# The opening of a fused attention, pooling and FFN block, ordered by a scheduler graph

## Chip, cores and metric

The kernel runs on one core of one Trainium2 chip. The metric is the device time of one execution in microseconds (us), as the median of several runs. TensorE is called PE in the profile, VectorE DVE, ScalarE ACT, GpSimd POOL and SyncE SP. DMAs are issued by SP and ACT here.

## The reference

One layer of a decoder block on x of 1024 rows (tokens) by 1024 columns, all in float32. What matters here is its start: a norm of x's rows, and one projection of the result, of which q and k are two parts (four heads, for each 128 columns of q and 128 of k).

```python
def rms_norm(x, g):
    xf = x.astype(jnp.float32)
    y = xf * lax.rsqrt(jnp.mean(xf * xf, axis=-1, keepdims=True) + NORM_EPS)
    return (y * g.astype(jnp.float32)).astype(x.dtype)
...
    u = rms_norm(h, mix_pre_g)
    z = jnp.einsum('bsd,de->bse', u, w_in)
    ...
    p, q, k, v = z[..., :o1], z[..., o1:o2], z[..., o2:o3], z[..., o3:o4]
    gate_a, gate_b = z[..., o4:o5], z[..., o5:]
    ya = jnp.einsum('bsc,cd->bsd', pool_mixer(p, pool_mix, pool_scale), w_branch_a)
    yb = jnp.einsum('bsc,cd->bsd',
                    diff_attention(q, k, v, lam_q1, lam_k1, lam_q2, lam_k2, subln_g, lambda_init),
                    w_branch_b)
    m = jax.nn.sigmoid(gate_a) * ya + jax.nn.sigmoid(gate_b) * yb
    h = h + rms_norm(jnp.einsum('bsd,de->bse', m, w_out), mix_post_g)
...
```

## The kernel before, in words

**Products.** A float32 operand is split into a rounded part (`hi`, on ACT) and the rest (`lo`, on DVE or POOL). A product is three matmuls: hi by hi, hi by lo, lo by hi. x is loaded in eight tiles of 128 rows (`xt`), normalised, transposed by PE (eight transposes of 128 by 128, `x_t`) and split. The rows are taken in two row blocks of 512 (tiles 0 to 3 and 4 to 7), the 1024 columns in two halves; so the transposed x is four operands, A11 and A12 (first row block, left and right half) and A21 and A22.

**Two forms.** Heads 0 and 1 are computed plainly (`common`): for each of q and k and each row block, eight pieces of the sum, each three matmuls. From head 2 on, q and k of a head make one *unit* of seven products instead of eight (`seven`), with sums of x's operands (S1 to S4, raw ones in `S_raw` and `A_raw`) and of the weights (T1 to T4, in `wf_t`). The accumulators of a unit are called Y, Z and X. After the units of q and k come those of v and p (`vp_unit`), the gates, and then a part ordered by a scheduler.

**The clockwork of the opening.** In `block_kernel`, the opening is written out by hand in the order in which each engine is to do it, under `tc.manual_schedule` for PE, ACT, DVE and POOL; DMAs on SP stand where the code calls them.

- `load_x`, and the gain vector `g1` as a load of 512 KB that copies it to all partitions. The order on SP is tile 0, gain, tile 1, weight 0, tile 2, weight 1, tiles 3 to 5, then weights 2 and 3 and tiles 6 and 7. Weights 0 to 3 are head 0's q and k, head 1's q and k.
- `square` (ACT, sum of squares of a row), `rstd` (DVE, then a `pow` on POOL), `normed` (DVE, one pass over 1024 columns), `turn` (PE).
- `turned_hi`, `turned_lo`, `turned_raw`: copies from PSUM to the operands.
- `first_hi`, `first_lo`: the split of a weight, the rest on POOL in four parts of 256 columns.
- `first_pair`: one of q, k of head 0 for two tiles, in matmuls of 256 columns. Head 1 is done later, in matmuls of 512 columns.
- `warm`: filler transposes, 40 ahead of x and 8 behind each of the first two tiles.
- `qk_done`: the result's split and its store from ACT's queue.

**The scheduler.** `Plan` holds tasks with an engine, a cost and a rank. `Plan.schedule` simulates them with costs written in the code and emits the order. Before, only the last part of the program used it. Tile pools decide which tiles share memory: `mm`, `fil` and `pair` are two PSUM buffers each (a `pair` has two banks).

Of the kernel before, what the change touches and what calls it, by code (L numbers as in the profile page):

```python
# [16 lines left out]
P = 128  # L17
# [28 lines left out]
RESERVE = {"E": 2, "gate": 2, "row": 2}  # L46
# [29 lines left out]
class Plan:  # L76
# [79 lines left out]
    def schedule(self, patience=None):  # L156
        patience = patience or {}
        free = {e: 0.0 for e in ("PE", "ACT", "DVE", "POOL", "SP")}
# [6 lines left out]
        for _ in range(len(self.tasks)):  # L165
# [41 lines left out]
            if e == "SP":  # L207
                dma_free = max(dma_free, t.end) + t.size / DMA_RATE
                t.landed = dma_free + DMA_LATENCY
# [14 lines left out]
    def emit(self):  # L224
        for t in self.order:
            for s in t.needs:
                if s.value is None:
                    s.value = s.make()
            t.fn()

# [694 lines left out]
def block_kernel(ctx, tc, x, w_in, pool_mix, pool_scale, w_branch_a, lam_q1, lam_k1, lam_q2,  # L925
# [192 lines left out]
    U = {n: operand(n) for n in ("A11", "A12", "A21", "A22")}  # L1118
    traws = {n: a8([P, 4, HALF], F32, n + "_raw") for n in ("A11", "A12", "S1", "S3")}
    traws["S2"], traws["S4"] = traws["A11"], traws["A12"]  # L1120
    g1 = wp.tile([P, D], F32, tag="wlo", bufs=2, name=name("g1"))
# [11 lines left out]
    def load_x(tb):  # L1133
        xt = b4([P, D], F32, "xt")
        nc.sync.dma_start(xt, x[tb * P:(tb + 1) * P, :])
        return xt

    def qk_done(h, e, t, src, st=None, stores=None):
        st = b4([P, 2, HALF], F32R, "qk_st") if st is None else st[e][:, :, half(t)]
# [11 lines left out]
        if stores is not None:  # L1151
            stores.extend(out_)
            return
        for o, s in out_:
            nc.scalar.dma_start(o, s)


    firsts = [(h, e) for h in range(2) for e in range(2)]
    plain, xts, xr = {}, [], []

    def first_raw(i):
        h, e = firsts[i]
        raw = raw_weights(w_cols((o_q, o_k)[e], h), ("wraw", "wraw", "whi", "whi")[i])
        plain[h, e] = raw.rearrange("p h k n -> p (h k) n"), b4([P, KD, P], F32R, "w_hi"), b4([P, KD, P], F32R, "w_lo")

    def first_hi(i):
        raw, hi, _ = plain[firsts[i]]
        nc.scalar.copy(hi, raw)

    def first_lo(i, part):  # L1170
        raw, hi, lo = plain[firsts[i]]
        k = slice(2 * part, 2 * part + 2)
        nc.gpsimd.tensor_tensor(out=lo[:, k], in0=raw[:, k], in1=f32(hi[:, k]), op=ALU.subtract)

    def common(h, e, t, o, c):
        _, hi, lo = plain[h, e]
        mac(o[:, c], [((hi[:, k, :], lo[:, k, :]),
                       tuple(a[:, k % 4, c] for a in U[f"A{t + 1}{k // 4 + 1}"])) for k in range(KD)])

    def square(tb):  # L1180
        ss = small(1, "ss")
        sumsq(xts[tb], ss)
        xr.append(ss)

    def rstd(tb):
        xr[tb] = rstd_of(xr[tb], 1, D)

    def normed(tb):
        nc.vector.scalar_tensor_tensor(out=xts[tb], in0=xts[tb], scalar=xr[tb], in1=g1, op0=ALU.mult, op1=ALU.mult)

    xts.append(load_x(0))
    nc.sync.dma_start(g1, mix_pre_g.partition_broadcast(P))
    xts.append(load_x(1))
    first_raw(0)
    xts.append(load_x(2))
    first_raw(1)
    for tb in range(3, 6):
        xts.append(load_x(tb))
    first_raw(2)
    lamt = temp("sg").rearrange("p (i d) -> p i d", d=HD)  # L1200
    o = [(fil("q"), fil("k")), (mm("q"), mm("k"))]

    def warm(n, src=ident):

        for i in range(n):
            k = i % (src.shape[-1] // P) * P
            nc.tensor.transpose(o[1][1][:, i % 4 * P:(i % 4 + 1) * P], src[:, k:k + P], ident)

    views = {}

    def first_pair(i, e):
        common(0, e, i // 2, o[i // 2][e], slice(i % 2 * 2 * P, (i % 2 + 1) * 2 * P))

    def turn(tb):
        both = pair("x_t")
        for k in range(KD):
            nc.tensor.transpose(both[:, k // 4, k % 4 * P:(k % 4 + 1) * P], xts[tb][:, k * P:(k + 1) * P], ident)
        cols = slice(tb % 4 * P, (tb % 4 + 1) * P)
        views[tb] = cols, [(both[:, kq, :].rearrange("p (k t) -> p k t", k=4),
                            [a[:, :, cols] for a in U[f"A{tb // 4 + 1}{kq + 1}"]]) for kq in range(2)]  # L1220

    def turned_hi(tb):
        for v, (hi, lo) in views[tb][1]:
            nc.scalar.copy(hi, v)

    def turned_lo(tb):
        for v, (hi, lo) in views[tb][1]:
            sub(lo, v, hi)

    def turned_raw(tb):  # L1230
        cols, ((v0, _), (v1, _)) = views[tb]
        for n, v in zip(("A11", "A12") if tb < 4 else ("S1", "S3"), (v0, v1)):
            nc.scalar.copy(traws[n][:, :, cols], v)

    def half_sums(b0, b1, *names):

        cols = slice((b0 - 4) * P, (b1 - 4) * P)
        a22, s1, s2, s4 = (traws[n][:, :, cols] for n in ("S3", "S1", "S2", "S4"))
        for n in names:
            if n == "S1":  # L1240
                tt(s1, s1, a22, ALU.add)
            elif n == "S2":
                tt(s2, s1, s2, ALU.subtract)
            elif n == "S3":
                tt(a22, a22, s2, ALU.subtract)
            else:
                tt(s4, s4, s2, ALU.subtract)

    with tc.manual_schedule(engines={nc.tensor.engine, nc.scalar.engine, nc.vector.engine, nc.gpsimd.engine}):
        warm(WARM)  # L1250
        square(0)
        rstd(0)
        normed(0)
        turn(0)
        warm(KD, xts[0])
        square(1)
        rstd(1)
        normed(1)
        turned_hi(0)
        first_hi(0)  # L1260
        first_lo(0, 0)
        first_lo(0, 1)
        turned_lo(0)
        turn(1)
        warm(KD, xts[1])
        xts.append(load_x(6))
        first_raw(3)
        xts.append(load_x(7))
        turned_hi(1)
        first_lo(0, 2)  # L1270
        first_lo(0, 3)
        turned_lo(1)
        square(2)
        rstd(2)
        normed(2)
        first_hi(1)
        first_lo(1, 0)
        square(3)
        rstd(3)
        for part in range(1, 4):  # L1280
            first_lo(1, part)
        turned_raw(0)
        turned_raw(1)
        for tb in range(2, NB):
            if tb == 2:
                first_pair(0, 0)
            turn(tb)
            if tb > 2:
                first_pair((tb - 2) // 2, (tb - 2) % 2)
            turned_hi(tb)  # L1290
            if tb + 1 < NB:
                normed(tb + 1)
            turned_lo(tb)
            if tb + 2 < NB:
                square(tb + 2)
                rstd(tb + 2)
            turned_raw(tb)
            if tb == 5:
                half_sums(4, 5, "S1", "S2")
            if tb == 6:  # L1300
                half_sums(4, 5, "S3", "S4")
            if tb == 7:
                half_sums(5, 6, "S1", "S2", "S3", "S4")
            if tb in (3, 5):
                first_hi(tb // 2 + 1)
                for part in range(4):
                    first_lo(tb // 2 + 1, part)
        stores = []

        def store():  # L1310
            while stores:
                nc.scalar.dma_start(*stores.pop(0))

        for e in range(2):
            qk_done(0, e, 0, o[0][e], stores=stores)
        first_pair(3, 0)
        first_pair(3, 1)
        half_sums(6, 8, "S1", "S2")
        U["S1"] = operand("S1")
        split(U["S1"], traws["S1"])  # L1320
        store()
        for e in range(2):
            qk_done(0, e, 1, o[1][e], stores=stores)
        U["S2"] = operand("S2")
        split(U["S2"], traws["S2"])
        store()
        W = weights(w_cols(o_q, 2), w_cols(o_k, 2))
        half_sums(6, 8, "S3", "S4")
        U["S3"] = operand("S3")
# [397 lines left out]
```

## Time and profile before

| | |
|---|---|
| median of 3 runs | 1251.7 us (1251.46 to 1251.93) |
| profiled execution | 1250.68 us |
| span of the profiled execution | 1248.9 us |
| PE busy | 99% of the span |
| DVE, ACT, POOL busy | 67%, 47%, 11% |

The span runs from the first to the last instruction in the trace. A row of a timeline names the start, the duration, the engine, the line, the operation, the tile written and those read, and in brackets how long the engine was idle before and what ended that. The ends of PE's matmuls are modelled, so pitches are taken from starts.

### The profile page before, as it was taken

The page shows a single profiled execution, that of the slowest core. Times are in us where ns is not written, and L with a number is a line of the kernel's source. Part 1 is how long each engine was busy: PE and PEld are TensorE (multiplying, and loading weights), DVE is VectorE, ACT ScalarE, POOL GpSimd, SP SyncE. Part 2 cuts the span into 40 slices and gives each one's busy share as a digit, 9 for nine tenths or more (in the row PEclk, how much of TensorE's full clock was granted, in tenths as well). Part 3 has the DMA queues.
Part 4 walks back from the last instruction along what each step waited for, and adds up shares of the span by engine and source line. Part 5 has one row for each costly group of instructions (what it writes and reads, how often), then busy time and mean ns, then how long its engine had stood idle before and what let it go on. Part 6 is the DMA issues. An engine that isn't in the chain of part 4 may idle for free.

```text
span 1248.9 us, 15724 instructions
## 1 busy us (share of the span) xinstructions
PE 1236.0 (99%) x5900; PEld 1037.7 (83%) x5900; DVE 839.2 (67%) x1314; ACT 583.5 (47%) x1051; POOL 142.5 (11%) x128
## 2 busy tenths in 40 slices
PE   8999999999999999999999999999999999999997
PEld 7878888888889998888888888888888888888886
DVE  5976776445399898895795655655655547955666
ACT  7543344434478773464553333333333333554552
POOL 4100000000201100010002111101111012000222
PEclk9999999999999999999999999999999999999999
DMA  8475336343593017572533332232333368733236
GB/s 254 149 235 192 139 120 220 105 133 118 213 389 139 18 59 269 196 264 90 168 136 101 110 126 88 90 117 86 127 108 103 105 211 284 242 96 107 79 108 211
DMA packets 139548, 190.69 MB, mean 153 GB/s; under 512 B 7632, under 2 KB 90320, under 8 KB 137040
## 3 DMA queue, kind: packets, MB, share of 16 engines
q1 hardware_dynamic: 127904, 159.15, 38.7%
q10 hardware_dynamic: 11568, 30.54, 6.5%
q8 instruction: 46, 0.75, 0.3%
q14 instruction: 30, 0.25, 0.1%
HBM read 128.06 MB, written 61.60 MB: 152 GB/s over the span
## 4 chain that ended last, share of the span: by engine, by line
PE 96%; ACT 1%; DVE 1%; DMA 0%; issue 0%; POOL 0%; SPq 0%; POOLq 0%; DVEq 0%; ACTq 0%
PE Y L1065 10%; PE Y L1066 10%; PE Y L1067 10%; PE X L1065 5%; PE X L1066 5%; PE X L1067 5%; PE Yd L1065 3%; PE Yd L1066 3%; PE Yd L1067 3%; PE Z L1066 3%; PE Z L1065 3%; PE Z L1067 3%; PE s L277 3%; PE o L277 3%; PE branch L1065 2%; PE branch L1067 2%
## 5 line engine op out<-in xcount | busy, mean ns | idle before, releaser
L1016 DVE TENSOR_TENSOR p<-Z,p 128x512 f32<-128x512 f32 x33 | 22.8, 691 | 165.5 <-PE Z L1067 161.8
L1065 PE MATMUL Y<-S_hi,Wh 128*128 128x512 f32 x288 | 112.3, 390 | 0.7 <-ACT p L1101 0.7
L1065 PE MATMUL X<-S_hi,Wh 128*128 128x512 f32 x288 | 112.3, 390 | 0.0
L1067 PE MATMUL Y<-S_hi,Wl 128*128 128x512 f32 x288 | 112.2, 389 | 0.0
L1066 PE MATMUL Y<-S_lo,Wh 128*128 128x512 f32 x288 | 112.1, 389 | 0.0
L1066 PE MATMUL X<-S_lo,Wh 128*128 128x512 f32 x288 | 112.0, 389 | 0.0
L1067 PE MATMUL X<-S_hi,Wl 128*128 128x512 f32 x288 | 112.0, 389 | 0.0
L1065 PE MATMUL Y<-A_hi,Wh 128*128 128x512 f32 x280 | 109.2, 390 | 0.0
L1066 PE MATMUL Y<-A_lo,Wh 128*128 128x512 f32 x280 | 109.1, 390 | 0.0
L1067 PE MATMUL Y<-A_hi,Wl 128*128 128x512 f32 x280 | 108.8, 389 | 0.0
L1034 ACT CAST Wh<-wf_t 128x1024 fp32r<-128x1024 f32 x66 | 68.6, 1053 | 68.2 <-PE Y L1066 32.8
L972 DVE TENSOR_TENSOR Wl<-wf_t,Wh 128x1024 fp32r<-128x1024 f32 x72 | 87.7, 1225 | 7.8 <-ACT Wh L1034 6.3
L972 DVE TENSOR_TENSOR w_op<-wd,w_op 128x512 fp32r<-128x512 f32 x77 | 56.7, 737 | 50.6 <-ACT w_op L1020 50.6
L1034 ACT CAST Wh<-w_raw 128x1024 fp32r<-128x1024 f32 x66 | 55.2, 837 | 67.9 <-PE Z L1066 38.0
L1020 ACT CAST w_op<-wd 128x512 fp32r<-128x512 f32 x77 | 47.9, 622 | 76.9 <-PE Yd L1067 36.7
L972 DVE TENSOR_TENSOR Wl<-w_raw,Wh 128x1024 fp32r<-128x1024 f32 x72 | 68.7, 954 | 16.4 <-ACT Wh L1034 14.6
L1065 PE MATMUL Yd<-w_op,s_op 128*128 128x512 f32 x176 | 68.6, 390 | 0.0
L1066 PE MATMUL Yd<-w_op,s_op 128*128 128x512 f32 x176 | 68.5, 389 | 0.0
L1067 PE MATMUL Yd<-w_op,s_op 128*128 128x512 f32 x176 | 68.3, 389 | 0.0
L1065 PEld LDWEIGHTS Y<-S_hi,Wh 128*128 128x128 f32 x288 | 54.1, 188 | 12.7 <-ACT p L1101 1.1
L1067 PEld LDWEIGHTS X<-S_hi,Wl 128*128 128x128 f32 x288 | 54.1, 188 | 11.2
L1067 PEld LDWEIGHTS Y<-S_hi,Wl 128*128 128x128 f32 x288 | 54.1, 188 | 11.2
(274 smaller groups left out, 3079.1 us busy)
## 6 DMA issues: line engine op xcount, KB each, us to landing
s_raw<-fsd SPq DMA_DIRECT2D x35, 512.0 KB, 3.6
w_raw<-in_w_in_dram SPq DMA_DIRECT2D x32, 512.0 KB, 4.1
w_raw<-in_w_ffn_gate_dram SPq DMA_DIRECT2D x22, 512.0 KB, 3.9
w_raw<-in_w_ffn_up_dram SPq DMA_DIRECT2D x22, 512.0 KB, 3.9
fsd<-fss SPq DMA_DIRECT2D x11, 1024.0 KB, 3.9
wd<-in_w_ffn_down_dram SPq DMA_DIRECT2D x44, 256.0 KB, 5.3
fsd<-F SPq DMA_DIRECT2D x33, 256.0 KB, 2.4
qd<-qk_st ACTq DMA_DIRECT2D x16, 512.0 KB, 4.0
```

The costliest lines, as they stand in the source:

```text
L277: nc.tensor.matmul(o, l, r, start=start, stop=stop, skip_group_check=skip)
L972: nc.vector.tensor_tensor(out=o, in0=a, in1=f32(hi), op=ALU.subtract)
L1016: nc.vector.tensor_tensor(out=o, in0=a, in1=b, op=op)
L1020: nc.scalar.copy(hi, a)
L1034: nc.scalar.copy(hi, a)
L1065: nc.tensor.matmul(o, ah, bh, start=start, stop=False, skip_group_check=goes_on)
L1066: nc.tensor.matmul(o, ah, bl, start=False, stop=False, skip_group_check=goes_on)
L1067: nc.tensor.matmul(o, al, bh, start=False, stop=stop, skip_group_check=goes_on)
```

## The change

The hand-written opening is replaced by a function `opening`, which builds a second `Plan` of all its steps, with ranks from tables of numbers (`RT`, `OFF`, `WRANK` and others), and emits the order that `schedule` makes of it. It also covers unit 2 and the weights of unit 3 (head 3). Its parts:

- **Loads**: tile 0, tile 1, weight 2 (head 1's q), tile 4, weight 3, weight 1, tiles 2, 3, 5, 7, weight 0, tile 6. The gain vector is loaded as 4 KB (8 by 128) from ACT's queue and transposed and spread by PE into two PSUM banks; from tile 2 on it is read from an SBUF copy.
- **First two tiles**: sum of squares in two halves (ACT and DVE), normalising and transposing in two halves.
- **POOL's pow** is planned as an operation that shares DVE's port (`port=True`).
- **First blocks**: head 1's q and k and head 0's are computed for the first tiles in separate passes (`PASSES`: all hi by hi, then hi by lo of x, then the weight's lo). Fillers: 10 first, then 14 placed by rank.
- **Second row block of heads 0 and 1**: in two banks that alternate, since Z and Y hold the others; Z's first three of four triples and Y's first product are placed early.
- **POOL** takes the S4 sum of tiles 4 to 6 (`S4E`) and two sums of head 3's weights (`FORMS`).
- The stores of q and k of heads 0 to 2 go from SP's queue; the four iotas and minima of `cnt` stand at the very start.

```diff
-RESERVE = {"E": 2, "gate": 2, "row": 2}
+RESERVE = {"E": 2, "gate": 2, "row": 2, "uw": 2}
...
+RT = (72, -300, -470, -138, -530, -42, 351, 625,)
...
+LOADS = (0, 1, 12, 4, 13, 11, 2, 3, 5, 7, 10, 6,)
...
+BLOCKS = ((0, 0, 0, 2,), (1, 0, 0, 2,), (0, 0, 2, 2,), (1, 0, 2, 2,), (0, 1, 0, 4,), (1, 1, 0, 4,),)
...
+PASSES = ("hh", "hl", "lh",)
+S4E = ("POOL", "POOL", "POOL", "DVE",)
+FORMS = (("DVE", "DVE", "DVE", "DVE",), ("POOL", "POOL", "DVE", "DVE",),)
...
+        pl.op("POOL", .55, lambda ms=ms, r=r: G.tensor_tensor(out=r(), in0=ms(), in1=k.mhalf[:, :1], op=ALU.pow), r=[ms], w=[r],
+              rank=R - 50, port=True)
...
+            e = S4E[c]
+            pl.op(e, dve(HALF) if e == "DVE" else 1.43, lambda: (V if e == "DVE" else G).tensor_tensor(
+                out=s4c(), in0=s4c(), in1=s2c(), op=ALU.subtract), r=[(r11, c)], w=[(r12, c)], rank=R + OFF[7], port=True)
...
+    os = {}
+    for rank, (h, t, c0, wide) in enumerate(BLOCKS):
+        if (h, t) not in os:
+            os[h, t] = [bank(("fil", "mm")[h], "qk") for _ in range(2)]
...
+    first.schedule(OPENING_PATIENCE, BEGIN)
+    with tc.manual_schedule(engines={e.engine for e in (nc.tensor, nc.scalar, nc.vector, nc.gpsimd, nc.sync)}):
+        first.emit()
...
-    with tc.manual_schedule(engines={nc.tensor.engine, nc.scalar.engine, nc.vector.engine, nc.gpsimd.engine}):
-        warm(WARM)
-        square(0)
-        rstd(0)
-        normed(0)
-        turn(0)
-        warm(KD, xts[0])
...
```

What this makes of the order. On PE, the start of the program before (`k_153` and later the fillers' bank; `x_t` is x transposed, `q_150` head 0's q):

```order
L1207 MATMUL k_153<-ident 128x128 x40
L1217 MATMUL x_t_203<-ident,xt_124 128x128 x8
L1207 MATMUL k_153<-ident,xt_124 128x128 x8
L1217 MATMUL x_t_234<-ident,xt_127 128x128 x8
L1207 MATMUL k_153<-ident,xt_127 128x128 x8
L991 MATMUL q_150<-A_hi_83,w_hi_131 128x256
L992 MATMUL q_150<-A_lo_84,w_hi_131 128x256
```

and in the changed program (`warm_123` is the fillers' bank, later that of the second tile's left half; `g_164` and `g_173` hold the spread gain, `qk_243` is head 1's q):

```order
L298 MATMUL warm_123<-ident 128x128 x10
L303 MATMUL warm_123<-ident,p_31_116 128x8
L313 MATMUL g_164<-ident,gT_157 128x128 x4
L313 MATMUL g_173<-ident,gT_157 128x128 x4
L316 MATMUL warm_123<-ident 128x128 x8
L359 MATMUL x_t_197<-ident,xt_114 128x128 x4
L316 MATMUL warm_123<-ident 128x128 x2
L359 MATMUL x_t_207<-ident,xt_114 128x128 x4
L316 MATMUL warm_123<-ident 128x128 x4
L359 MATMUL warm_123<-ident,xt_118 128x128 x4
L359 MATMUL x_t_232<-ident,xt_118 128x128 x4
L502 MATMUL qk_243<-A_hi_212,w_hi_202 128x256 x4
```

The fillers are fewer and split, the gain vector passes through PE, the tiles are transposed in halves, and the first matmuls use the rounded parts alone.

On DVE, the start before (`ms` is the mean square, `cnt` a table of the pooling part, `g_13_95` the gain in SBUF):

```order
L1008 TENSOR_SCALAR ms_198<-ss_196 128x1
L1458 TENSOR_SCALAR cnt<-cnt 128x16
L1189 SCALAR_TENSOR_TENSOR xt_124<-xt_124,rstd_199,g_13_95 128x1024
L1008 TENSOR_SCALAR ms_222<-ss_220 128x1
L1458 TENSOR_SCALAR cnt<-cnt 128x16 x3
L1189 SCALAR_TENSOR_TENSOR xt_127<-xt_127,rstd_223,g_13_95 128x1024
```

and in the changed program (`xt_114` is the first tile, `xt_118` the second; ISA is the half sum of squares and the read of its sum):

```order
L417 ISA junk,ss_159<-xt_114 128x512
L417 ISA ss_159 128x1
L420 TENSOR_SCALAR ms_171<-ss_159 128x1
L417 ISA junk,ss_180<-xt_118 128x512
L417 ISA ss_180 128x1
L436 SCALAR_TENSOR_TENSOR xt_114<-xt_114,rstd_178,g_164 128x512
L420 TENSOR_SCALAR ms_191<-ss_180 128x1
L436 SCALAR_TENSOR_TENSOR xt_114<-xt_114,rstd_178,g_173 128x512
L436 SCALAR_TENSOR_TENSOR xt_118<-xt_118,rstd_195,g_164 128x512
L436 SCALAR_TENSOR_TENSOR xt_118<-xt_118,rstd_195,g_173 128x512
```

The second tile's half sum stands ahead of the first tile's normalising.

On DVE, around the store steps of the second row block before (`q_739` and `k_740` are head 1's q and k of that block, each in a bank of its own):

```order
L972 TENSOR_TENSOR S_lo_673<-S_raw_94,S_hi_672 128x2048
L1144 SCALAR_TENSOR_TENSOR qk_st_702<-q_676,qk_st_702 128x512
L972 TENSOR_TENSOR qk_st_729<-k_677,qk_st_729 128x512
L972 TENSOR_TENSOR S_lo_733<-A_raw_92,S_hi_732 128x2048
L1144 SCALAR_TENSOR_TENSOR qk_st_790<-q_739,qk_st_790 128x512
L972 TENSOR_TENSOR qk_st_795<-k_740,qk_st_795 128x512
```

and in the changed program (`qk_666` is head 0's q, `qk_711` head 1's q; `qk_747`, head 0's k, takes the bank of `qk_666`, and `qk_790`, head 1's k, that of `qk_711`):

```order
L283 TENSOR_TENSOR A_raw_249<-S_raw_525,A_raw_249 128x4x128
L1354 TENSOR_TENSOR Wl_705<-wf_t_472,Wh_687 128x1024
L1354 TENSOR_TENSOR S_lo_709<-S_raw_525,S_hi_702 128x2048
L1354 TENSOR_TENSOR S_lo_728<-A_raw_249,S_hi_707 128x2048
L481 SCALAR_TENSOR_TENSOR qk_st_724<-qk_666,qk_st_724 128x512
L283 TENSOR_TENSOR S_raw_572<-x_t_631,A_raw_249 128x4x128
L387 TENSOR_TENSOR A_raw_271<-A_raw_271,A_raw_249 128x4x128
L481 SCALAR_TENSOR_TENSOR qk_st_764<-qk_711,qk_st_764 128x512
```

Two rests of 2048 columns now stand ahead of the step that frees the bank. On POOL, the sums that were DVE's are these rows of the changed program:

```order
L387 TENSOR_TENSOR A_raw_271<-A_raw_271,A_raw_249 128x4x128 x3
L555 TENSOR_TENSOR wf_t_743<-w_raw_339 128x512
L555 TENSOR_TENSOR wf_t_743<-w_raw_339,w_raw_455 128x512
```

From unit 3's second product on the order of the instructions is that of before on every engine, up to the names.

More of the change, by code (lines that the diff above doesn't have):

```diff
@@ L154, in room, with schedule @@
         return at
-    def schedule(self, patience=None):
+    def schedule(self, patience=None, begin=None):
         patience = patience or {}
-        free = {e: 0.0 for e in ("PE", "ACT", "DVE", "POOL", "SP")}
+        free = {e: (begin or {}).get(e, 0.0) for e in ("PE", "ACT", "DVE", "POOL", "SP")}
         waiting = {t: len(t.before) for t in self.tasks}
@@ L1131, in w_cols, with qk_done @@
         return w_in[:, o + i * P:o + (i + 1) * P]
[L1133 to L1139, printed above, removed]
+    def qk_done(h, e, t, src, st):
+        st = st[e][:, :, half(t)]
         hi, lo = st[:, 0], st[:, 1]
@@ L1166, in first_hi @@
[L1166 to L1198, printed above, removed]
@@ L1199, in block_kernel @@
-    first_raw(2)
-    lamt = temp("sg").rearrange("p (i d) -> p i d", d=HD)
[L1201 to L1220, printed above, removed]
@@ L1249, in block_kernel @@
-    with tc.manual_schedule(engines={nc.tensor.engine, nc.scalar.engine, nc.vector.engine, nc.gpsimd.engine}):
-        warm(WARM)
-        square(0)
-        rstd(0)
-        normed(0)
-        turn(0)
-        warm(KD, xts[0])
[L1256 to L1329, printed above, removed]
-        split(U["S3"], traws["S3"])
-        o = fil("q"), fil("k")
-        for e in range(2):
-            common(1, e, 0, o[e], slice(0, HALF))
-            qk_done(1, e, 0, o[e], stores=stores)
-        U["S4"] = operand("S4")
-        split(U["S4"], traws["S4"])
-        store()
-        o = mm("q"), mm("k")
-        for e in range(2):
-            common(1, e, 1, o[e], slice(0, HALF))
@@ L1341, in block_kernel @@
-    for e in range(2):
-        qk_done(1, e, 1, o[e])
+    lamt = temp("sg").rearrange("p (i d) -> p i d", d=HD)
+    first = Plan()
+    U, W, st = opening(first, SimpleNamespace(
+        nc=nc, a8=a8, b4=b4, mm=mm, fil=fil, pair=pair, small=small, wp=wp, name=name, f32=f32, triple=triple, temp=temp,
+        sub=sub, junk=junk, mhalf=mhalf, ident=ident, cnt=cnt, x=x, g=mix_pre_g, qd=qd, kd=kd, AF=AF,
+        qk_cols=lambda h, e: w_cols((o_q, o_k)[e], h)))
+    first.schedule(OPENING_PATIENCE, BEGIN)
@@ L1344, in block_kernel @@
+    with tc.manual_schedule(engines={e.engine for e in (nc.tensor, nc.scalar, nc.vector, nc.gpsimd, nc.sync)}):
+        first.emit()
+    U = {n: (hi(), lo()) for n, (hi, lo) in U.items()}
+    W = {n: (hi()[:, i], lo()[:, i]) for n, (hi, lo, i) in W.items()}
+    late = st[0]()
     later = []
```

373 lines of the change are left out of this document (323 added, 50 removed).

## The prediction

> **What bounds the kernel now.** I read the head of the page first, then the chain of work that ended last, then TensorE's waits over the whole span, then windows of the opening and of a later stretch.
>
> ```profile
> span 1248.9 us, 15724 instructions
> PE 1236.0 (99%) x5900; PEld 1037.7 (83%) x5900; DVE 839.2 (67%) x1314; ACT 583.5 (47%) x1051; POOL 142.5 (11%) x128
> PE 96%; ACT 1%; DVE 1%; DMA 0%; issue 0%; POOL 0%; SPq 0%; POOLq 0%; DVEq 0%; ACTq 0%
> ```
>
> TensorE (PE) is busy for 99% of the span and is 96% of the chain. Its waits, then two windows (us, busy time of PE, weight loads, DVE, ACT and POOL, clock, DMA):
>
> ```profile
> PE x_t L1217 <- DVE xt L1189: 2.9, 2, 1.6
> PE k L1207 <- POOL ident masks.py:199: 1.4, 1, 1.4
> PE q L992 <- DVE A_lo L972: 1.3, 2, 0.8
> PE Y L1065 <- ACT p L1101: 0.7, 1, 0.7
> PE x_t L1217 <- ACT A_raw L1233: 0.3, 1, 0.3
> 7.80:25.00 17.20, 13.19 (x108) 12.29 (x108) 12.18 (x21) 14.76 (x27) 9.19 (x13) 1.00 1.11 349
> 87.00:187.00 100.00, 100.00 (x453) 81.84 (x453) 70.82 (x107) 40.09 (x60) 0.00 (x0) 1.00 0.47 159
> ```
>
> The larger waits are all for the opening's tiles (x, q, Y). From 87 us on PE has no idle time, from 7.8 to 25 it has 4. So only the opening can give anything, and what a change there is worth is how much earlier PE reaches a point behind which both programs have the same instructions. My marker is the first matmul of the third head-pair unit's second product, X, at 89.99 us. PE's timeline (start, duration, name, [idle before, releaser]):
>
> ```profile
> 7.82 1.09 PE L1217 MATMUL x_t<-ident,xt 128*128 128x128 f32 x8
> 13.11 0.38 PE L991 MATMUL q<-A_hi,w_hi 128*128 128x256 f32 x1
> 14.32 0.39 PE L992 MATMUL q<-A_lo,w_hi 128*128 128x256 f32 x1 [0.83 <-DVE A_lo L972]
> 14.66 0.27 PE L991 MATMUL q<-A_hi,w_hi 128*128 128x256 f32 x1
> 17.04 0.28 PE L993 MATMUL q<-A_hi,w_lo 128*128 128x256 f32 x1
> 23.82 1.03 PE L1217 MATMUL x_t<-ident,xt 128*128 128x128 f32 x8
> 24.61 0.36 PE L991 MATMUL q<-A_hi,w_hi 128*128 128x256 f32 x1
> 67.24 0.39 PE L1065 MATMUL X<-S_hi,Wh 128*128 128x512 f32 x1
> 72.68 0.39 PE L1065 MATMUL Y<-A_hi,Wh 128*128 128x512 f32 x1
> 89.99 0.39 PE L1065 MATMUL X<-S_hi,Wh 128*128 128x512 f32 x1
> ```
>
> Starts of queued instructions give the pitch: 8 transposes from 23.82 to 24.61, 0.099 each; 20 matmuls of 256 columns from 14.66 to 17.04, 0.119 each; 24 of 512 columns from 67.24 to 72.68, 0.227 each. Up to the marker both programs hold 64 transposes of x, 192 matmuls of 256 columns and 192 of 512 columns: 6.3 + 22.8 + 43.5 = 72.6 us. What the marker has beyond that, 89.99 - 72.6 = 17.4 us, is lost: 7.8 before x's first transposes, 5.2 of the listed waits that lie behind them, the rest (4.4) filler transposes and restarts. The forecast is this loss worked out again for the new order.
>
> **First transposes of x.**
>
> ```profile
> 4.47 1.06 ACT L1013 ACTIVATE junk<-xt 128x1024 bf16<-128x1024 f32 x1 [2.46 <-DMA xt<-in_x_dram]
> 6.48 1.28 DVE L1189 SCALAR_TENSOR_TENSOR xt<-xt,rstd,g 128x1024 f32<-128x1024 f32 x1 [0.59 <-POOL rstd L1009]
> 1.19 0.42 SPq L1192 DMA_DIRECT2D g<-in_mix_pre_g_dram  x1
> g<-in_mix_pre_g_dram SPq DMA_DIRECT2D x1, 512.0 KB, 5.1
> 1.66 0.42 SPq L1135 DMA_DIRECT2D xt<-in_x_dram  x1
> xt<-in_x_dram SPq DMA_DIRECT2D x1, 512.0 KB, 6.2
> L1016 DVE TENSOR_TENSOR p<-Z,p 128x512 f32<-128x512 f32 x33 | 22.8, 691 | 165.5 <-PE Z L1067 161.8
> psc<-in_pool_scale_dram SPq DMA_DIRECT2D x1, 2.0 KB, 2.6
> ```
>
> The order keeps x's first two tiles ahead of all, but the second load is now the second tile, not the gain vector, so it lands where the second did: 1.19 + 5.1 = 6.3 (the third, issued at 1.66, landed at 7.9). The first lands at 4.47 as before. VectorE (DVE) has the second tile's half sum of squares queued ahead of the first tile's normalising, so that early half waits for 6.3. The half sum on DVE isn't in the trace; ends: half of ACT's 1.06 (0.5) and ACT's whole 1.06; I take 0.7, from the row with as many elements on the same engine (0.69). Then half of 1.28: 6.3 + 0.7 + 0.65 = 7.7. **7.7 instead of 7.8**: halving the work is eaten by the wait. The gain vector, 4 KB now, passes through PE and lands in two PSUM banks; by the one small transfer of the trace (2.6 us from its issue) it is there at 3.5, and spread by PE before 6.5, under cover of the wait for the tile. If it took 5.1 as the large one did it would cost 1.0; that stays in the range.
>
> **First matmuls.**
>
> ```profile
> 9.97 1.05 ACT L1168 CAST w_hi<-w_raw 128x1024 fp32r<-128x1024 f32 x1
> 16.46 2.05 ACT L1233 COPY A_raw<-x_t 128x512 f32<-128x512 f32 x4
> 9.06 4.10 SPq L1040 DMA_DIRECT2D w_raw<-in_w_in_dram  x2
> w_raw<-in_w_in_dram SPq DMA_DIRECT2D x2, 512.0 KB, 9.9
> ```
>
> The first weight is now the third load: 7.9, cast by 8.9 (1.05), then on ACT four pieces of 0.5 (2.05 for 4) up to the second tile's first half: 10.9, first matmul at 11.1. From 7.7 that is 3.4, of which the 16 transposes of two tiles are 1.6 of work: **1.8 lost**. Before, the first matmul stood at 13.11 and the next waited until 14.32. Now all passes with the rounded part of x come first, then those with its rest, then those with the weight's rest, so DVE's rests (0.7 each behind ACT's pieces, the second tile's first by 11.6, wanted at 12.1) and GpSimd's (4 x 0.735 from 8.9: 11.9, wanted at 13.0) stand ready.
>
> Then 72 matmuls of 256 columns and 8 transposes follow: 11.1 + 8.6 + 0.8 = 20.5. Next is head 0's q, whose weight is the 11th load. In the trace two loads at this place were issued from 9.06 on over 4.10 us and took 9.9: 19.0 to 23; the pace of loads (6.3, 7.9: 1.6 each) gives 4.47 + 10 x 1.6 = 20.5. With half its cast (0.5) behind it: 21.2 or so, **0.7 lost** (0 to 1.9). GpSimd's pow is waited for by DVE's normalising alone (idle 0.59 and 0.66 before 6.48 and, below, 15.59); with PE's 72 matmuls in hand that is covered, and where the scheduler now puts it gives nothing, at the best 0.6.
>
> **Second row block.** PE goes on from 21.2: 120 x 0.119 = 14.3, 40 transposes 4.0, 9 + 12 + 24 + 24 wide matmuls 15.6, restarts 0.6. Head 0's k of the second row block starts at 55.7. It uses the bank in which head 0's q stood, because the unit's product Z holds the other, and so waits for DVE's store step of that q.
>
> ```profile
> 65.70 2.28 DVE L972 TENSOR_TENSOR S_lo<-S_raw,S_hi 128x2048 fp32r<-128x2048 f32 x1
> 15.59 1.84 DVE L1189 SCALAR_TENSOR_TENSOR xt<-xt,rstd,g 128x1024 f32<-128x1024 f32 x1 [0.66 <-POOL rstd L1009]
> L1173 POOL TENSOR_TENSOR w_lo<-w_raw,w_hi x16: 723/735/1711, 11.1 to 37.0; 128x256 fp32r<-128x256 f32 x16
> L1519 POOL TENSOR_TENSOR fss<-F 128x512 f32<-128x512 f32 x11 | 17.1, 1553 | 176.6 <-DVE F L1016 140.6 <-DVE F L280 36.0
> ```
>
> The last x transposes end at 42, ACT's copies of the last tile at 45.8, DVE's last sum for S1 at 46.4, S1's rounding on ACT 1.9 later at 48.6. DVE then has two rests of 2.2 and the store step of 0.7 ahead: 53.7, so 2.0 before PE wants the bank. But two sums of head 3's weights now run on GpSimd in that stretch, 2 x 1.553 = 3.1. The same normalising took 1.28 alone and 1.84 beside GpSimd's w_lo, and one w_lo took 1.711 rather than 0.735: the two engines hold each other up. The stall lies between 0 and 3.1 - 2.0 = 1.1: **0.5 lost**. Head 1's k, 24 matmuls (5.4) later, waits likewise for head 1's q, two short steps (1.9) behind: no stall.
>
> The Trainium skill (SBUF — State Buffer, "Who interferes with whom") has VectorE and GpSimd share a port pair under an exclusive lock, where the later comer stands still for the whole instruction. The trace agrees in kind: 1711 ns is about 735 plus most of a 1.28 us step. By that rule alone, all 3.1 would come on top, a stall of 1.1.
>
> **What costs nothing.** The stores of q and k go from ACT's queue to SP's, ahead of loads that the chain needs near 100 us; "DMA 0%; issue 0%" in the chain and PE's unbroken 87 to 187 speak for slack of tens of us. Head 3's weights are prepared earlier under the same cover. The iotas and minima stand before the first tile lands at 4.47, where DVE and GpSimd have nothing else. Restarts between short groups, which nothing above counts: 1.0 in all, the 0.6 included.
>
> **The sum.** 7.7 + 1.8 + 0.7 + 0.5 + 1.0 = 11.7 lost, against 17.4: the marker comes 5.7 earlier, say 5.6. The profiled execution took 1250.68 (its span and 1.8 around it) and would take 1245.1; the median of the runs is 1251.7, 1.0 above it, so **1246.1**. With every bound at its good or bad end the gain is 4 to 7, 1244.7 to 1247.7.
>
> **The rivals.** *The clock comes late.* PE's warm-up (us, busy PE, weight loads, clock, DMA):
>
> ```profile
> 1.40:3.40 2.00, 1.98 (x10) 1.99 (x11) 1.00 0.72 178
> 5.40:7.80 2.40, 2.40 (x23) 2.24 (x21) 1.00 0.93 312
> ```
>
> Transposes took 0.2 us for the first 2 us and 0.104 in the last 2.4, whatever the clock column says: some 4 us of unbroken filler were needed for the double rate. Now 10 fillers replace 40, with holes for the gain vector. If the rate is gained only on the first matmuls, 4 us of them run at half and 2 us are lost: 1248.1. Against it: PE stood idle for x (2.9, the longest 1.6) and for q (up to 0.8) before 14.66 and still ran 0.119 from there. Chance 0.09.
>
> By the Trainium skill (TensorE: Matmul & The Clock Gate, Part 4) a transpose does not count as busy for the gate, so fillers would be worth nothing, this rival certain, and the time 1248.1. The trace speaks against it: the rate doubled with nothing but transposes run.
>
> *VectorE held by all five sums.* If GpSimd's three sums of x's tiles push the chain as well, 5 x 1.553 = 7.8 less 2.0 of slack is 5.8 at most; midway between that and 1.1 stands a stall of 3.5, 3.0 over mine: 1249.1. For it, the locks above; against it, the three start while DVE waits for ACT. Chance 0.08.
>
> *The wait only moves.* If a queue behind the second load (first weight later than 11.1, head 0's q at 23 or more) takes up most of the gain, under 2.5 us is left: about 1251, the change not doing what its order says. Chance 0.05.
>
> *Slower: PE at half rate through the first matmuls.* Were the thin warm-up followed by groups of four with gaps, so that the double rate never came while x's first half is worked on (11 to 28 us), the 112 or so matmuls of 256 columns there would take 0.11 more each (0.2 against 0.104 is 1.9 times, and 0.119 x 0.9 = 0.11): 12.3 us, 1258.4. Some 50 slow ones eat the gain; from 74 (another 2.5 us) it is slower by over 0.2%. Against it stands the 0.119 after those stalls. Chance 0.04.
>
> **How the numbers follow.** My forecast 0.70, a gain of more than 7 another 0.04. A measurement of this kernel tells about 0.2% (2.5 us) from no change. Faster by more: 0.70 + 0.04 + 0.09 + half of the second rival (it ends right at 2.5) = 0.87; within: 0.04 + 0.05 = 0.09; slower 0.04. The range takes in the forecast's bounds and the first two rivals: 1244.5 to 1249.3.
>
> **What would show it.** In the new trace: x's first transposes at 7.7; first matmul of 256 columns at 11.1, the next without a wait; a wait of under 1.9 for head 0's first weight near 20.5; one of under 1.1 for DVE's store step near 55.7; the marker, the first X matmul of unit 3's second product, at 84.4; behind it no idle time on PE. Matmuls of 256 columns at 0.2 after 11 would show a clock rival; DVE's 2048-column rests at over 4 us, the held VectorE; a marker at or behind 88, that the loss stayed.

## The result, and the profile after

The changed kernel took 1246.87 us (median of 6 runs, 1246.27 to 1248.11) against 1251.58 for the kernel before on the same chip: a ratio of 0.9964, with a 95% interval from 0.9951 to 0.9977. That is 4.7 us faster, where 1246.1 was forecast. The head of its page and its chain:

```profile
span 1244.7 us, 15702 instructions
PE 1234.3 (99%) x5877; PEld 1035.8 (83%) x5877; DVE 842.9 (68%) x1324; ACT 580.2 (47%) x1047; POOL 151.0 (12%) x129
PE 97%; DVE 1%; DMA 1%; SPq 1%; ACT 0%; issue 0%; POOLq 0%; DVEq 0%; ACTq 0%
```

The profiled execution took 1246.5, 4.2 less than that of before, and the span is 4.2 shorter. TensorE's waits over the whole span, and the window that had 4 us of idle time before (same columns as there):

```profile
PE warm L298 <- POOL ident masks.py:199: 1.4, 1, 1.4
PE qk L502 <- DVE qk_st L481: 1.1, 1, 1.1
PE qk L502 <- ACT A_hi L365: 0.8, 1, 0.8
PE qk L502 <- ACT w_hi L456: 0.5, 1, 0.5
PE g L313 <- ACT gT L304: 0.3, 1, 0.3
```

```profile
7.80:25.00 17.20, 15.92 (x132) 15.33 (x130) 13.73 (x22) 15.21 (x27) 13.56 (x17) 1.00 1.11 338
```

PE is busy for 15.9 us of that window instead of 13.2. The waits for x's transposes and for x's rests (2.9 and 1.3) are gone; in their place are three waits of q and k that the old order didn't have. PE's timeline at the places of the prediction, the marker last:

```profile
7.72 0.60 PE L359 MATMUL x_t<-ident,xt 128*128 128x128 f32 x4
11.06 1.23 PE L502 MATMUL qk<-A_hi,w_hi 128*128 128x256 f32 x8 [0.77 <-ACT A_hi L365]
12.12 1.12 PE L502 MATMUL qk<-A_lo,w_hi 128*128 128x256 f32 x8
21.39 1.26 PE L502 MATMUL qk<-A_hi,w_hi 128*128 128x256 f32 x8 [0.51 <-ACT w_hi L456]
57.53 0.50 PE L502 MATMUL qk<-A_hi,w_hi 128*128 128x512 f32 x1 [1.13 <-DVE qk_st L481]
85.59 0.39 PE L1447 MATMUL X<-S_hi,Wh 128*128 128x512 f32 x1
```

The marker stands at 85.59 instead of 89.99, 4.4 earlier; nearly all of it arrives at the end.

### The profile page after: what moved, and what is told of

Read it like the earlier page. It is cut to its first block, busy times and chain, and to the rows that moved or that the text cites. A ratio compares the mean times of both kernels' runs of the same rounds, so it can differ in the third digit from the quotient of the medians.

```text
span 1244.7 us, 15702 instructions
## 1 busy us (share of the span) xinstructions
PE 1234.3 (99%) x5877; PEld 1035.8 (83%) x5877; DVE 842.9 (68%) x1324; ACT 580.2 (47%) x1047; POOL 151.0 (12%) x129
## 4 chain that ended last, share of the span: by engine, by line
PE 97%; DVE 1%; DMA 1%; SPq 1%; ACT 0%; issue 0%; POOLq 0%; DVEq 0%; ACTq 0%
PE Y L1447 10%; PE Y L1448 10%; PE Y L1449 10%; PE X L1447 5%; PE X L1448 5%; PE X L1449 5%; PE Yd L1447 3%; PE Yd L1448 3%; PE Yd L1449 3%; PE Z L1447 3%; PE Z L1449 3%; PE Z L1448 3%; PE s L659 3%; PE o L659 3%; PE branch L1447 2%; PE branch L1449 2%
## 5 line engine op out<-in xcount | busy, mean ns | idle before, releaser
L1416 ACT CAST Wh<-wf_t 128x1024 fp32r<-128x1024 f32 x62 | 64.4, 1053 | 62.8 <-PE Y L1448 32.8
L1416 ACT CAST Wh<-w_raw 128x1024 fp32r<-128x1024 f32 (+1 forms) x62 | 51.9, 836 | 63.6 <-PE Z L1448 37.5
```

The lines of the kernel that those rows point to most:

```text
L1416: nc.scalar.copy(hi, a)
```

## The experiments

All but two of them (E7, E8) keep the changed kernel's order of tasks and change only what is named, so that a marker can be laid to the edit; the planner, given other costs, would write the whole order anew. Ratios are to the kernel before on the same chip; E1 to E8 ran on one chip, E9 to E11 on another.

| run | marker, us | median, us | ratio and 95% interval |
|---|---|---|---|
| changed kernel | 85.59 | 1246.87 | 0.9964 (0.9951 to 0.9977) |
| E6, the same again | 85.49 | 1246.71 | 0.9969 (0.9956 to 0.9981) |
| E1, weight sums on VectorE | 84.19 | 1246.05 | 0.9959 (0.9944 to 0.9973) |
| E2, no fillers | 84.59 | 1247.24 | 0.9974 (0.9964 to 0.9983) |
| E3, gain vector as 512 KB | 87.95 | 1249.34 | 0.9987 (0.9977 to 0.9996) |
| E4, no passes | 87.26 | 1248.82 | 0.9984 (0.9975 to 0.9993) |
| E5, four edits | 83.70 | 1245.01 | 0.9956 (0.9944 to 0.9969) |
| E7, products late | 88.53 | 1250.06 | 0.9994 (0.9985 to 1.0003) |
| E8, pow not planned | 88.89 | 1249.00 | 0.9983 (0.9973 to 0.9992) |
| E9, three edits | 83.46 | 1244.51 | 0.9951 (0.9939 to 0.9964) |
| E10, all sums on VectorE | 84.00 | 1246.11 | 0.9962 (0.9949 to 0.9975) |
| E11, stores from ScalarE | 85.47 | 1247.55 | 0.9974 (0.9962 to 0.9985) |

**E1: the two weight sums on VectorE.**

```diff
-lambda e=e, o=o, a=a, b=b: (V if e == "DVE" else G).tensor_tensor(
+lambda e=e, o=o, a=a, b=b: V.tensor_tensor(
```

> The changed kernel with its order kept; the two sums of head 3's weights (128x512 each) run on VectorE, behind its store step of head 0's q, not on GpSimd. Theory (the port holds VectorE): its two 2048-column rests take 2.2 to 2.3 us, not 3.4 each, the store step stands at 54.6 instead of 56.8, TensorE's wait of 1.13 us for it goes, and the marker (first X matmul of unit 3's second product) moves from 85.59 to 84.5; time about 1245.7 against 1246.9. Rival (the rests are slow for another reason, or the wait only moves to head 1's k or to the S products): rests stay at 3.4 or a new wait of about 1 us stands behind 57 us; marker 85.5, time 1246.9.

VectorE (first two rows: the rests; third: the store step) and GpSimd's sums in the changed kernel, then VectorE in E1:

```profile
50.17 3.40 DVE L1354 TENSOR_TENSOR S_lo<-S_raw,S_hi 128x2048 fp32r<-128x2048 f32 x1
53.49 3.38 DVE L1354 TENSOR_TENSOR S_lo<-A_raw,S_hi 128x2048 fp32r<-128x2048 f32 x1
56.80 0.68 DVE L481 SCALAR_TENSOR_TENSOR qk_st<-qk,qk_st 128x512 fp32r<-128x512 f32 x1
50.13 1.30 POOL L555 TENSOR_TENSOR wf_t<-w_raw 128x512 f32<-128x512 f32 x1 [1.97 <-DVE Wl L1354]
51.38 3.34 POOL L555 TENSOR_TENSOR wf_t<-w_raw,w_raw 128x512 f32<-128x512 f32 x1
```

```profile
50.26 2.29 DVE L1354 TENSOR_TENSOR S_lo<-S_raw,S_hi 128x2048 fp32r<-128x2048 f32 x1
52.47 2.28 DVE L1354 TENSOR_TENSOR S_lo<-A_raw,S_hi 128x2048 fp32r<-128x2048 f32 x1
54.67 0.68 DVE L481 SCALAR_TENSOR_TENSOR qk_st<-qk,qk_st 128x512 fp32r<-128x512 f32 x1
84.19 0.39 PE L1447 MATMUL X<-S_hi,Wh 128*128 128x512 f32 x1
```

The rests fall from 3.4 to 2.29 each, the store step stands at 54.67 as expected, and PE's wait is gone. The two engines had held each other: the second sum took 3.34 where the first took 1.30. So this part of the change costs time. The marker's 1.4 is that wait of 1.13 and the slow start of the matmuls behind it; the median falls by 0.8, which is within the scatter of the runs.

**E2: one filler transpose in place of 24.**

```diff
-for i in range(WARM0)], w=[bw], rank=-2000)
+for i in range(1)], w=[bw], rank=-2000)
...
-lambda i=i: nc.tensor.transpose(bw()[:, i % 4 * P:(i % 4 + 1) * P], k.ident, k.ident),
+lambda: None,
```

> The changed kernel with its order kept, but 1 filler transpose in place of 24. Theory of the clock rival (TensorE's rate doubles only after some us of unbroken work): transposes of x still run at 0.2 us, the first matmul stays near 11, and the first 4 us of matmuls run at 0.22 a piece, not 0.12: about 2 us lost, 0.5 of it taken from the wait for head 0's first weight; marker near 87.1, time 1248.4. Rival (fillers only stand in the way of x's transposes): first transposes at 7.1 instead of 7.72, first matmul at 10.6 instead of 11.06 and at 0.12 each; the wait for head 0's weight grows by as much; marker 85.4 to 85.6, time 1246.8.

PE in this run:

```profile
7.31 1.97 PE L359 MATMUL x_t<-ident,xt 128*128 128x128 f32 x8 [1.58 <-DVE xt L436]
10.94 1.48 PE L502 MATMUL qk<-A_hi,w_hi 128*128 128x256 f32 x8
12.25 1.12 PE L502 MATMUL qk<-A_lo,w_hi 128*128 128x256 f32 x8
84.59 0.39 PE L1447 MATMUL X<-S_hi,Wh 128*128 128x512 f32 x1
```

Neither expectation held in full. x's own transposes now run at the slow rate (8 from 7.31 to 9.08, 0.22 each), but the first eight matmuls take 1.31 from start to start instead of 1.06, and the next eight 0.95. That is 0.25 us lost, not 2, and not shown to be the clock's: the third and fourth of the eight follow at 0.12 each already, and the 0.25 lies in the steps to the fifth and sixth (0.27 and 0.22). The marker is 1.0 earlier although the first matmul moved by only 0.1; the wait for head 0's weight is missing in this run, where the others with the same loads and first blocks (E1, E6, E7, E10, E11) have 0.3 to 1.0. The median says that it makes no difference that can be told. The fillers are worth about nothing here, in either direction.

**E3: the gain vector as one 512 KB load again, between the first two tiles.**

```diff
             nc.sync.dma_start(xt[tb](), k.x[tile_cols(tb), :])
+            if tb == 0:
+                nc.sync.dma_start(g1(), k.g.partition_broadcast(P))
```

> The changed kernel with its order kept, but the gain vector is again one 512 KB load copied to all partitions, issued between the first two tiles; its transposes through TensorE and its copies are gone. Theory (each load in line costs its 1.6 us): second tile lands at 7.3 instead of 5.7, first weight at 9.6 instead of 8.0, first matmul at 12.4, head 0's first weight at 22.3; marker 87.1, time 1248.4. Rival (the loads are not what the first matmuls wait for): first matmul within 0.3 of 11.06, marker within 0.4 of 85.6, time 1246.9.

PE's wait for x, then its timeline:

```profile
PE x_t L363 <- DVE xt L439: 4.3, 1, 4.3
```

```profile
9.38 1.12 PE L363 MATMUL x_t<-ident,xt 128*128 128x128 f32 x4 [4.25 <-DVE xt L439]
14.16 1.59 PE L505 MATMUL qk<-A_hi,w_hi 128*128 128x256 f32 x8
```

The window from 10 to 20 us in E3 (columns as above; the clock is the third number from the end):

```profile
10.00:20.00 10.00, 10.00 (x66) 9.75 (x65) 8.11 (x13) 7.90 (x13) 7.70 (x9) 0.76 1.10 355
```

The theory holds for the first weight (in use at 9.63), but the second tile is in use only at 7.96, and the whole size was too small: the first matmul is 3.1 later, not 1.4, the marker 2.4 and the time 2.5. Behind PE's 4.25 us of idle time x's transposes run at 0.21 to 0.23 each and stand in the way, which the expectation left out; the granted clock of the window is 0.76, where the changed kernel has 1.00. How the 3.1 divides between the loads and the slow transposes is not shown. The load order with the small gain vector is the largest part of the change that was undone by itself in the unchanged order.

**E4: the three passes undone.**

```diff
+                if ph in ("hh", "hl"):
+                    return
                 todo = [(w[i]()[:, 4 * q + kk, :], a()[:, kk, cs]) for n, w, a in (
...
-                    ("hh", wh, hi), ("hl", wh, lo), ("lh", wl, hi)) if ph in (n, "all")]
+                    ("hh", wh, hi), ("hl", wh, lo), ("lh", wl, hi)) if ph in (n, "all", "lh")]
```

> The changed kernel with its order kept, but the first blocks' three passes are undone: each block does hi by hi, hi by lo and lo by hi piece by piece, at the place of its last pass. Theory (the passes let TensorE start on the rounded parts): the first matmul waits for the rests, GpSimd's of the weight at 11.9 and VectorE's of the second tile at 12.3, so it stands at 12.2, head 1's k waits another 0.4 for VectorE's rest of its weight (15.5), 0.5 is taken from the wait for head 0's first weight; marker 86.7, time 1248.0. Rival (the start is set by loads alone): marker within 0.3 of 85.6, time 1246.9.

PE's waits that are new, then the marker:

```profile
PE x_t L359 <- ACT A_raw L376: 1.3, 1, 1.3
PE qk L504 <- DVE w_lo L1356: 0.5, 1, 0.5
PE qk L504 <- DVE A_lo L1356: 0.3, 1, 0.3
```

```profile
87.26 0.39 PE L1449 MATMUL X<-S_hi,Wh 128*128 128x512 f32 x1
```

The wait for the weight's rest comes as expected (0.5). That for x's rest is 0.3 only: the first matmul stands at 11.02, not at 12.2. And a wait of 1.3 comes that was not expected: a later tile's transposes wait for ScalarE to empty their bank. Marker 1.7 later (1.1 expected), time 1.9.

**E7: unit 2's products behind all of heads 0 and 1** (planned anew).

```diff
-            pl.op("PE", TRIPLE, fn, r=[hi, lo, *U[un]], w=[o], rank=rank)
+            pl.op("PE", TRIPLE, fn, r=[hi, lo, *U[un]], w=[o], rank=rank, behind=last[0])
```

> The changed kernel, planned anew with unit 2's products held behind all of heads 0 and 1, so that each q and k of the second row block has a bank of its own and nothing of Y and Z stands between the transposes of the last two tiles. Theory (the early products cover the last tiles' splitting on ScalarE and VectorE): TensorE waits 2 to 3 us near 40 to 44 for the split of the last tile, and saves the 1.13 of the shared bank; marker 87.1, time 1248.4. Rival (the shared banks were a loss, the cover not needed): marker 84.5, time 1245.8.

PE's timeline, with the marker, then the window from 40 to 50 us in the changed kernel and in E7:

```profile
41.95 0.50 PE L502 MATMUL qk<-A_hi,w_hi 128*128 128x512 f32 x1 [0.90 <-ACT A_hi L365]
43.49 0.59 PE L502 MATMUL qk<-A_lo,w_hi 128*128 128x512 f32 x1 [1.04 <-DVE A_lo L1354]
43.87 0.63 PE L502 MATMUL qk<-A_hi,w_lo 128*128 128x512 f32 x1
46.86 0.54 PE L502 MATMUL qk<-A_hi,w_hi 128*128 128x512 f32 x1
88.53 0.39 PE L1447 MATMUL X<-S_hi,Wh 128*128 128x512 f32 x1
```

```profile
40.00:50.00 10.00, 10.00 (x50) 8.31 (x49) 8.98 (x14) 6.79 (x10) 1.62 (x1) 1.00 0.46 154
```

```profile
40.00:50.00 10.00, 8.06 (x30) 6.22 (x31) 9.45 (x16) 6.33 (x9) 1.60 (x1) 0.83 0.32 117
```

With no products to do, PE waits for the last tile's split, 1.9 us. What the expectation left out comes behind that: from 43.87 to 46.86 there are seven matmuls at 0.43 each, where 0.23 is the pitch elsewhere, and the granted clock of the window is 0.83, not 1.00. By that clock the 10 us lose another 1.7. The wait for the shared bank is gone, and the marker is 2.9 later, not 1.5. The shared bank is the price of the early products, and by far the smaller of the two.

**E8: pow not counted as a user of the port** (planned anew).

```diff
-              rank=R - 50, port=True)
+              rank=R - 50)
```

> The changed kernel, planned anew with GpSimd's pow not counted as a user of VectorE's port. Theory (the planner's rule only shifts places, pow is covered by TensorE's matmuls in hand): marker 85.6 within 0.7 of the changed kernel, time 1246.9 within 0.7. Rival (pow beside VectorE's normalising holds both up): normalising steps of 1.8 us instead of 1.28, a wait of TensorE for a tile's transposes of 1 us or more, marker 86.6 or later, time 1248 or more.

PE's waits for ScalarE, VectorE's normalising of two tiles, and the marker:

```profile
PE qk L502 <- ACT A_hi L365: 2.4, 3, 1.5
```

```profile
18.59 2.48 DVE L436 SCALAR_TENSOR_TENSOR xt<-xt,rstd,g 128x1024 f32<-128x1024 f32 x2 [0.39 <-POOL rstd L427]
88.89 0.39 PE L1447 MATMUL X<-S_hi,Wh 128*128 128x512 f32 x1
```

The theory fell. The rival's marker and time came (3.3 later, 1249.0), but not by its mechanism: no normalising step of 1024 columns is slower for it (at most 1.63, in the changed kernel 1.72). The planner simply wrote another order: there the last tile's transposes stand without products behind them, and PE waits as in E7 (1.5 and 1.1), with a granted clock of 0.83 from 40 to 50 us as there. What the planning of pow brings here is the order that comes out, not a port kept free. Whether other ranks would bring the same order without it was not tried.

**E5, E6 and E9: the waits that were left.** E5 is E1 with three more edits: no fillers between the transposes of the first two tiles, head 0's first weight loaded ahead of tile 7, and the first copy of the gain vector behind the second tile's rounded parts. E6 is the changed kernel once more, in the same rounds. E9 is E5 without the last of these edits.

```diff
+    for late_, early_ in ((("g", 0), ("hi", 1, 1)), (("x", 7), ("w", 0, 0))):
+        t_ = first.tag[late_]
+        first.order.remove(t_)
+        first.order.insert(first.order.index(first.tag[early_]) + 1, t_)
```

> The changed kernel with four edits of its order, aimed at the waits that its profile still shows: the two weight sums on VectorE (as in the run before), no fillers between the transposes of the first two tiles (18 in place of 24), the first copy of the gain vector on ScalarE behind the second tile's rounded parts, and head 0's first weight loaded one place earlier (tenth, ahead of tile 7). Theory (each wait named by the trace is worth its length): TensorE's wait of 1.13 at the second row block goes, 0.5 for head 0's weight goes, the first matmul comes 0.45 earlier (10.6); marker 83.5 instead of 85.59, time 1244.8. Rival (the gain is given back further on, where VectorE waits for loads near 480 us): marker 83.5, but the stretch behind it 1 us longer, time 1245.8 to 1246.

> The changed kernel itself, on the same chip and in the same rounds as the kernel with the edits, for comparison: marker 85.6 within 0.3, time 1246.9 within 0.6. If the marker moves by more than that, landing times of the loads differ from run to run by as much as the edits are worth.

> The kernel with the edits, with the first copy of the gain vector back at its place ahead of the second tile's rounded parts. Theory (the first matmul's PSUM bank is the one that holds the left half of the gain, so its copy must come out first; moving it back made the first matmul wait until 11.36): first matmul at 10.65, no other wait over 0.6 up to the marker, marker 83.1, time 1244.4. Rival (the first matmul waits for the second tile's rounded part only): first matmul at 11.1 to 11.4 again, marker 83.7, time 1245.0.

The first matmul in E5, E6 and E9, then E9's marker:

```profile
11.36 1.22 PE L503 MATMUL qk<-A_hi,w_hi 128*128 128x256 f32 x8 [1.26 <-ACT g L432]
```

```profile
10.82 1.24 PE L502 MATMUL qk<-A_hi,w_hi 128*128 128x256 f32 x8 [0.38 <-ACT A_hi L365]
```

```profile
10.85 1.23 PE L503 MATMUL qk<-A_hi,w_hi 128*128 128x256 f32 x8 [0.50 <-ACT A_hi L366]
83.46 0.39 PE L1448 MATMUL X<-S_hi,Wh 128*128 128x512 f32 x1
```

E6 gave 85.49 and 1246.71, as expected. E5 reached its forecast (83.70 and 1245.0 for 83.5 and 1244.8) by luck in part, since one of its edits was a mistake: the first matmul came at 11.36, not at 10.6. In E5 it waits for the copy of the gain vector, since the bank it writes is the one that held the gain's left half. With the copy back in its place (E9) the first matmul is at 10.85 again and q and k have two waits left, together 0.8. E9 is the fastest version here, 0.9951 of the kernel before, 6.1 us; beside the changed kernel in E6 its marker is 2.0 earlier. E5's rival came in part: the stretch behind its marker is 0.7 longer than in the changed kernel (see the last section). The intervals of E9 and of the changed kernel overlap, so by the times alone it is not shown to be faster than the changed kernel.

**E10: all five sums on VectorE.**

```diff
-            pl.op(e, dve(HALF) if e == "DVE" else 1.43, lambda: (V if e == "DVE" else G).tensor_tensor(
+            pl.op(e, dve(HALF) if e == "DVE" else 1.43, lambda: V.tensor_tensor(
```

> The changed kernel with its order kept; all five sums that went to GpSimd run on VectorE: the two of head 3's weights as in the first experiment, and the three S4 sums of tiles 4 to 6 (0.6 us each, 1.8 in all, between 34 and 46 us). Theory (these three cost VectorE nothing on GpSimd, and relieve it where the chain to the store step is tight): the store step stands 0.6 to 1.8 later than in the first experiment (54.67), TensorE waits 0 to 1.1 for it near 56; marker 84.2 to 85.6, time 1246 to 1247. Rival (they hold VectorE as the other two do): the marker as in the first experiment or earlier, 84.2 or less, time 1246.0 or less.

VectorE's store step and the marker:

```profile
55.09 0.68 DVE L481 SCALAR_TENSOR_TENSOR qk_st<-qk,qk_st 128x512 fp32r<-128x512 f32 x1
84.00 0.39 PE L1447 MATMUL X<-S_hi,Wh 128*128 128x512 f32 x1
```

The store step is 0.4 later than in E1 (0.6 to 1.8 expected), within its slack, and the marker is where E1's was, as the rival had it. The three S4 sums on GpSimd neither cost nor bring anything.

**E11: the stores back on ScalarE's queue.**

```diff
-            pl.op("SP", .4, lambda: nc.sync.dma_start(k.kd[h][:, :, half(t)], f32(st(None))), r=keys, rank=rank, size=.524)
+            pl.op("SP", .4, lambda: nc.scalar.dma_start(k.kd[h][:, :, half(t)], f32(st(None))), r=keys, rank=rank, size=.524)
...
-                pl.op("SP", .4, lambda i=i: nc.sync.dma_start(k.qd[h][i][:, :, half(t)],
+                pl.op("SP", .4, lambda i=i: nc.scalar.dma_start(k.qd[h][i][:, :, half(t)],
```

> The changed kernel with its order kept, but the stores of q and k of heads 0 to 2 issue from ScalarE's queue again, each at its place in the order. Theory (a store waits for VectorE's rest of the same q or k, and in ScalarE's queue the casts behind it wait with it): S1's and S2's rounding stands 1 us or more later, TensorE's wait of 1.1 at the second row block grows to 2 or more; marker 86.6 or later, time 1248 or more. Rival (the queue is of no account, as the prediction had it): marker within 0.3 of 85.5, time 1246.8.

The marker is at 85.47 and PE's wait at the second row block is 1.1 as before the edit. My theory here was wrong and the prediction's line right: the queue of the stores is of no account for TensorE here. The median, 1247.55, is 0.7 above the changed kernel's, within the scatter of the runs.

## Why the prediction was right, point by point

**The bound.** It held that only the opening could give anything, and that the gain is the marker's shift. The marker moved by 4.4, the profiled execution by 4.2.

**First transposes, 7.7: measured 7.72, for another reason; that the number fits is luck.** The second tile was in use at 5.70 rather than 6.3, and its half sum takes 0.69 as assumed:

```profile
5.70 0.69 DVE L417 CUSTOM_DVE_ANT_0 junk<-xt 128x512 bf16<-128x512 f32 x1 [0.29 <-DMA xt<-in_x_dram]
6.32 0.74 DVE L436 SCALAR_TENSOR_TENSOR xt<-xt,rstd,g 128x512 f32<-128x512 f32 x1
6.03 1.85 PE L316 MATMUL warm<-ident 128*128 128x128 f32 x8
```

The first half tile is ready at 7.1, but PE is then still in its eight fillers. It cost nothing, since ScalarE is behind:

```profile
8.01 1.05 ACT L456 CAST w_hi<-w_raw 128x1024 fp32r<-128x1024 f32 x1 [1.52 <-DMA w_raw<-in_w_in_dram]
9.92 0.60 ACT L431 COPY g<-g 128x512 f32<-128x512 f32 x1
20.72 1.14 ACT L456 CAST w_hi<-w_raw 128x512 fp32r<-128x512 f32 x2 [1.69 <-DMA w_raw<-in_w_in_dram]
```

**First matmul, 11.1: 11.06.** The weight is there at 8.0 and its cast is followed by four pieces, as worked out. **Head 0's first weight, forecast to land at 20.5 with a loss of 0.7 (0 to 1.9): in use at 20.72, loss 0.51.**

**Second row block, 0.5 lost (0 to 1.1): 1.13.** This is the term that was mis-sized. The chain was right (the wait, its releaser, and the two rests of 2.2 that grow), but both numbers of its subtraction were too large. Each rest lost 1.1 to a sum, 2.2 together and not up to 3.1; the first sum took 1.30, not 1.553. And the slack was 1.05, not 2.0: S1's last sum on VectorE ended at 48.2 instead of 46.4, so the rests began at 50.17 instead of 48.6, and PE wanted the bank at 56.40 (57.53 less the wait) instead of 55.7. In E1, where no sum holds the rests, the store step ends at 55.35, which is that 1.05. 2.2 less 1.05 is the wait to within 0.1.

The rows of E1's section show the rule of the Trainium skill at work (SBUF — State Buffer, "Who interferes with whom"): one engine stands still while the other holds the shared port. The second sum starts inside the first rest and takes 3.34, and the second rest starts inside that sum and takes 3.38. That the prediction's wait by this rule, 3.1 less 2.0, is 1.1 too is chance, since both were about 0.9 too large.

**Restarts, 1.0: about 1.8.** The prediction gave no row for its 1.0. From 11.06 to 21.39 there are 9.4 of work in 10.3, from 21.39 to 57.53 there are 33.9 in 36.1, from 57.53 to the marker 27.9 in 28.1. Less the waits of 0.51 and 1.13 that leaves 0.5, 1.1 and 0.2. These two terms, 0.6 and 0.8 too small, less the 0.2 saved at head 0's weight, are the 1.2 by which the marker came later than the 84.4 forecast.

**The rivals.** The clock rival did not come, and E2 shows that the fillers were not what kept it away: even there, with slow transposes, the first matmul came at 10.94 and the first eight lost 0.25, not 2. The Trainium skill (TensorE: Matmul & The Clock Gate, Part 4) has transposes not count for the clock gate. The changed kernel's trace speaks against it: TensorE had run nothing but transposes when the pitch fell from 0.21 (the eight fillers from 6.03 to 7.72) to 0.11 (the four transposes from 7.72 to 8.16). Half rate as such is real, though: it came back in E3, E7 and E8, each time behind waits of TensorE. VectorE held by all five sums: E10 shows that the three for x's tiles hold nobody up, as the prediction held against it. The other two had nothing behind them in the changed kernel's trace.

**What was covered.** The stores (E11) cost nothing, as said. That planning pow would give nothing, at the best 0.6, was wrong: without it the order is another and the marker 3.3 later (E8).

**Where the gain comes from.** Taken away one at a time, the small gain vector is worth 2.4 at the marker (E3), the passes 1.7 (E4) and the early products 2.9 (E7); against them the weight sums on GpSimd cost 1.4 (E1). The three add up to more than the 4.4 gained, so they are not shares of it. Two of them hold time at half rate behind new waits (granted clock 0.76 and 0.83 in the windows of E3 and E7), which the kernel before doesn't lose: its clock is 1.00 from 7.8 to 25 us and no window up to its marker is lower. The halves of the first two tiles were not tried alone.

## What to carry to other kernels

When one engine is busy for 99% of the span, find a point behind which nothing changes, and count what is lost ahead of it; most pieces of that loss can then be forecast from pitches and landings of the old trace. A sum moved to GpSimd is not free for VectorE: look at what two-input step VectorE has queued in that stretch, and count nearly the whole sum (here 1.1 of 1.30 each time). Behind a new wait of TensorE look at the granted clock too: in E7 1.9 us of waiting brought 1.7 us of half rate with it. And before moving a copy out of the way, ask whose bank it empties.

## What the runs showed that I had not expected

The stretch from the marker to TensorE's last matmul isn't the same in all profiles, though its order is: 1152.2 us before (1242.21 - 89.99), 1152.4 in the changed kernel, 1152.6 in E6 and E11, but 1153.1 to 1153.8 in the other nine. In six of the nine (not in E7, E8 and E9) part of it is a wait of 0.2 to 0.3 for a step of VectorE that works on the gates' loads near 495 us, here in E1:

```profile
PE branch L1447 <- DVE sgs L662: 0.2, 1, 0.2
```

Set matmul by matmul beside the kernel before, most of the difference arises between 480 and 547 us in eight of the nine; E7 has half of it earlier, around a wait of 0.54 at 102.84. The lower mean clocks (0.997 in E3 and E7, 1.000 before) are not its cause: they come from the stretches ahead of the marker, and from 90 to 1200 us the granted clock is 1.00 in every run. What sets the rest is open; it is the reason why the markers tell the edits apart better than the times do.

A 128x512 sum on GpSimd took from 1.30 to 3.34 us in one and the same kernel, according to what VectorE held.
